# Reordering the small matmuls of a chunked recurrence on TensorE: one row size at a time, heads and blocks in turn

## The chip, the cores and the metric

The kernel runs on one core of one Trainium2 chip. The metric is the time of one execution in microseconds (us) on the device; lower is better. All times below are of this one core.

## What is computed

One layer of a hybrid decoder for 1024 prompt tokens and 8 sample tokens. What matters here is mixer B, a recurrence over tokens for 8 heads of 64 (the reference, cut):

```python
def wkv7_scan(r, decay, k, v, kk, a, S0):
    def step(S, inp):
        r_t, d_t, k_t, v_t, kk_t, a_t = inp
        sa = jnp.einsum('bhvk,bhk->bhv', S, -kk_t)
        S = S * d_t[:, :, None, :] + sa[..., None] * (kk_t * a_t)[:, :, None, :] + v_t[..., None] * k_t[:, :, None, :]
        y = jnp.einsum('bhvk,bhk->bhv', S, r_t)
        return S, y
```

Around it stand a projection `h @ w_in`, a second mixer (gated by a 128x128 matrix per head), `@ w_out`, a cross attention over 256 memory tokens and a squared-relu feed-forward, all in float32.

## The kernel before

Phase 1 (until about 780 us) makes the projections and both mixers, phase 2 the rest. All large products go through one helper, `gemm` (line 132): float32 is split into a high and a low part, and three exact-part matmuls of 128x128 weights by 256 to 512 columns are issued per 128 rows of the contraction; these have the output `ps_g` or, for the memory, `ps_kv`.

The recurrence is done by chunks of 64 tokens, in two halves of 512 tokens, for pairs of heads: a head lies on 64 partitions, a pair on 128. Per half there are four pairs; two pairs (`q`) share an inverse and a chain. The parts, all plain float32, so that each matmul in the code is two passes in the trace (two weight loads and two MATMUL records):

- `gram` (line 494, output `psgram`): products of the factors inside each chunk; weights 64 rows x 128 columns.
- `inverse` and `join` (lines 574 to 597, `ps_j`): a DVE routine inverts 16x16 blocks, then five sets of 32x32x32 products join them to 64x64. Each of four blocks b lies on 32 partitions; `tile_position` puts it on that part of the array. 224 matmuls per join, four joins.
- `fold` (line 609, `psf`): 64x64x64 products with the inverse, 8 chunks x 2 heads per call, 16 calls.
- `chain` (lines 622 and 630, `psx`, `psz`): the recurrence itself, chunk by chunk, two matmuls of 128 rows x 64 columns per head and chunk with copies by ACT and DVE between; not touched.
- `outs` (lines 647 and 648, `psy`): per chunk and head one matmul with 128 rows of weights (line 647) and one with 64 rows (line 648) into the same 64x64 of PSUM; 128 of each in the program.

The list `ORDER` sets the priority of these parts. The order on each engine is then laid out by the framework's scheduler, so that parts run into each other on PE, which executes its matmuls in that order. The small matmuls' outputs lie in PSUM pools of two buffers: `pm` (gram, join and others) and `py` (fold, outs, one product of join and others).

Of the kernel before, what the change touches and what calls it, by code (L numbers as in the profile page):

```python
# [9 lines left out]
F32 = mybir.dt.float32  # L10
# [6 lines left out]
PSUM = bass.MemoryType.PSUM  # L17
DRAM = bass.MemoryType.DRAM

P = 128  # L20
# [42 lines left out]
def order():  # L63
    """phase 1 in the order in which its parts take precedence: names and arguments (half, pair or head, part)."""
    parts = (p.split() for p in ORDER.replace("\n", " ").split(","))
    return [(name, *map(int, args)) for name, *args in parts]


class K:
# [25 lines left out]
    # ---------------------------------------------------------------- helpers  # L95
# [14 lines left out]
    def load_w(self, src, g=None, eng=None, st=None):  # L110
        """src: [1024, 128] of DRAM (or st: loaded) -> hi and lo [128, 8, 128]."""
        nc = self.nc
        st = st or self.w_tile(src)
        if g is not None:
            nc.gpsimd.tensor_tensor(st, st, g.unsqueeze(2).broadcast_to([P, KT, P]), op=ALU.mult)  # L115
        wh = self.wp.tile([P, KT, P], F32R, tag="wh", name="wh")
        wl = self.wp.tile([P, KT, P], F32R, tag="wl", name="wl")
        self.split(wh, wl, st, eng=eng or nc.gpsimd)
        return wh, wl

    def gemm(self, ps, w, xh, xl, cols, kt=KT):
        """ps += w^T x over kt tiles, in three exact-part passes."""
# [11 lines left out]
    def rsqrt_small(self, out, ss, scale, eps, shape, pool):  # L134
        """out = 1/sqrt(ss*scale + eps): a first guess from the exponent's bits, three Newton steps."""
# [12 lines left out]
    def rsqrt(self, v, y, t):  # L148
        """v -> 1/sqrt(v) in y (v [128, n] kept); t: scratch."""
# [81 lines left out]
    # ---------------------------------------------------------------- phase 1  # L231
# [34 lines left out]
    def x_store(self, hf, i):  # L266
        """tile i of 128 tokens: x^T to d_x (of the second half, ahead of its turn, with the sum of squares)."""
# [19 lines left out]
    def x_scale(self, rs, c0):  # L287
        """rb from column c0 on: 1 / rms (a column of rs per tile of tokens) over the partitions."""
# [65 lines left out]
    def proj(self, hf, col0, dst, sdst):  # L354
        """dst[128, 512] (and sdst[128, 8]) = rstd * (x g)^T w_in columns, for the half's tokens."""
# [13 lines left out]
    def shifted(self, hf, mi, out):  # L369
        """out[128, 512]: projected rows of m-tile mi after the token shift."""  # L370
# [11 lines left out]
    def loras(self, hf, i):  # L382
        """inputs of the decay and a low-rank maps (i = 0), of the gate's (1)."""
# [18 lines left out]
    def rkv(self, hf, pr, i):  # L402
        """r, k or v (i) of a pair of heads."""
# [5 lines left out]
    def kknorm(self, hf, pr):  # L409
        """unit-norm removal keys of both heads of the pair."""  # L410
# [12 lines left out]
    def lora(self, ps, fs, i):  # L423
        """the decay's (i = 0) or a's low-rank map: its input's high and low parts lie in one tile's halves."""
# [4 lines left out]
    def decay(self, hf, pr):  # L429
        """per-chunk cumulative decays lam, their inverses il, and tanh of the a-gate."""  # L430
# [22 lines left out]
    def factors(self, hf, pr):  # L453
        """decay-scaled factors: st = [-kk lam | r lam], bk = [kk a / lam | k / lam], and the bonus."""
# [21 lines left out]
    def gram(self, hf, pr):  # L476
        """masked products of the factors inside each chunk."""
# [9 lines left out]
        for cg in range(2):  # L487
            for h in range(2):
                hr = slice(64 * h, 64 * h + 64)
                orr = slice(64 - 64 * h, 128 - 64 * h)  # L490
                psg = self.pm.tile([P, 4, P], F32, tag="m", name="psgram")
                for ci in range(4):
                    c = cg * 4 + ci
                    nc.tensor.matmul(psg[:, ci, :], bk[hr, c].rearrange("p j t -> p (j t)"), st[hr, c, h, :], start=True, stop=True)  # L494
                cc = slice(cg * 4, cg * 4 + 4)
# [14 lines left out]
    def values(self, hf, pr):  # L510
        """values by token zv, with the state in the chain's first chunk."""
# [14 lines left out]
    def ends(self, hf, pr):  # L526
        """chunk-end factors e by token, in the place of the chunks' bk."""
# [11 lines left out]
    def inverse(self, hf, q):  # L539
        """(I - N)^-1 of the diagonal 16x16 blocks of two pairs, one problem per partition."""  # L540
# [18 lines left out]
    def join(self, hf, q):  # L559
        """16x16 -> 32x32 -> 64x64 inverses: D + D L D with L the blocks above the diagonal ones."""  # L560
# [23 lines left out]
        ps3 = self.py.tile([P, NS, 32], F32, tag="y", name="ps_j3")  # L584
        for h in range(2):
            r1, r2 = rows[2 * h], rows[2 * h + 1]
            for c in range(NS):
                nc.tensor.matmul(ps3[r2, c, :], wj[r2, c, :], nb[r2, c, :], start=True, stop=True, tile_position=(64 * h + 32, 64 * h + 32))
            self.copy(("vector", "scalar")[h])(dt[r2], ps3[r2])
            for c in range(NS):  # L590
                ab = self.s[prs[c // NCH]]["ab"]
                nc.tensor.matmul(ps2[r2, c, :], ab[r1, c % NCH, 32:64], tt[r1, c, 0:32], start=True, stop=True, tile_position=(64 * h, 64 * h + 32))
            self.copy("scalar" if h else "vector")(wj[r2], ps2[r2])
        for h in range(2):
            r2 = rows[2 * h + 1]
            for c in range(NS):
                nc.tensor.matmul(ps3[r2, c, :], dt[r2, c, :], wj[r2, c, :], start=True, stop=True, tile_position=(64 * h + 32, 64 * h + 32))
            nc.vector.tensor_copy(tt[r2, :, 0:32], ps3[r2])

    def fold(self, hf, pr, i):  # L600
        """the inverse's product with the chunk-end factors (i = 0) or the outputs' ones (1), in their place."""
# [3 lines left out]
        for h in range(2):  # L605
            hr = slice(64 * h, 64 * h + 64)
            dst = t["e"][hr, 0:NCH, h, :] if i == 0 else t["ab"][hr, :, C:]
            for c in range(NCH):
                nc.tensor.matmul(ps[hr, c, :], tt[hr, c, :], dst[:, c, :], start=True, stop=True)  # L609
            self.copy((("vector", "scalar"), ("scalar", "scalar"))[i][h])(dst, ps[hr])  # L610

    def chain(self, hf, q, c0, c1):
        """chunks c0..c1 of the recurrence of two pairs."""
# [21 lines left out]
    def outs(self, hf, pr):  # L635
        """the recurrence's outputs by token, less their mean over each head."""
# [16 lines left out]
    def gn_core(self, y, n, sq, rs, pool, tag):  # L653
        """y -> (y - mean) / sqrt(var + eps) over the 64 partitions of each head."""
# [34 lines left out]
    # ---------------------------------------------------------------- sample tokens of mixer B  # L689
# [124 lines left out]
    # ---------------------------------------------------------------- mixer A  # L814
# [16 lines left out]
    def layernorm(self, x, n, rows, h):  # L831
        """x [rows, n, 128] normalised in place over the last axis; h: the head of the n groups (None: one each)."""
# [23 lines left out]
    def proj_a(self, hf, h, i):  # L856
        """v (i = 0) or u (1) of head h, before the gelu; the gelu of both after u."""
# [54 lines left out]
    # ---------------------------------------------------------------- states out, memory keys and values  # L912
# [17 lines left out]
    def mem_norm(self):  # L930
        """normalised memory tokens, feature-major, to d_m."""
# [30 lines left out]
    def memkv(self, i, m0, m1):  # L962
        """feature tiles m0..m1 of the memory's keys (i = 0) or values (1)."""
# [21 lines left out]
    # ---------------------------------------------------------------- phase 2  # L985
# [3 lines left out]
    def tile_cols(i):  # L989
        """columns of the i-th tile of 128 prompt tokens; tile 8: the sample tokens."""  # L990
# [5 lines left out]
    def halves(self, b0, b1):  # L996
        """the half of x (hi, lo) with columns b0..b1, and their slice in it."""
# [3 lines left out]
    def residual(self, m, x, b0, b1, first):  # L1001
        """x (columns b0..b1 of feature tile m) -> hi and lo; adds x^2 to the sums."""
# [10 lines left out]
    def phase2(self, phases):  # L1013
# [5 lines left out]
        with ExitStack() as c2:  # L1019
            # each pool lies on the bytes of one of phase 1 (o0: sb, x0: xp, x1: sa), and waits for that one alone  # L1020
# [62 lines left out]
    def token_ms(self, tiles, pool):  # L1083
        """sums of squares by token, in the columns of a PSUM tile."""
# [5 lines left out]
    def token_rs(self, tiles):  # L1090
        """1 / (16 rms) by token, in columns of rs (sample tokens: rs8)."""
# [16 lines left out]
    def attention(self, h, grps):  # L1108
        """head h of the cross attention for groups of 256 prompt tokens (with group 1: the sample tokens)."""
# [54 lines left out]
    def softmax(self, ps, n, scale, pool):  # L1164
        """rows of ps [n, 256]: softmax(ps * scale), scale > 0 (an AP [n, 1] or 1.0)."""
# [12 lines left out]
    def sample_head(self, h, qs):  # L1178
        """head h of the cross attention of the sample tokens over their cached memories."""
# [182 lines left out]
```

## Time and profile before

| | us |
|---|---|
| median of 3 runs | 1934.5 (1933.2 to 1941.1) |
| span of the profiled execution, first to last instruction | 1928.3 |
| what lies around the span, against the median | 6.2 |
| PE busy | 1837.6 (95%) |
| DVE busy | 1027.4 (53%) |
| ACT busy | 634.2 (33%) |
| POOL busy | 631.0 (33%) |

No device time of the profiled execution itself is on its page beside the span, so the span stands for it, and the 6.2 us to the median for what lies around it. A matmul's record runs from its start to the modelled end of its result, so records of neighbours overlap, and the step from one start to the next is what a matmul takes from the engine. Idle time is listed with what ended it.

### The profile page before, as it was taken

To read this page: it belongs to the slowest core of one execution; us is meant where nothing else is said; L and a number is where in the kernel's file an instruction comes from. 1 tells how busy PE (TensorE), PEld (TensorE's weight loads), DVE (VectorE), ACT (ScalarE), POOL (GpSimd) and SP (SyncE) were. 2 spreads that over 40 slices of the span, in tenths; PEclk is the share of its full clock that TensorE was granted. 3 is DMA by queue.
4 is the path that set the end of the run, shared out by engine and by line. 5 is a ranking of instruction groups with operands and counts; after the bars stand their busy time and mean duration, and the time that the engine had idled before them with its cause. 6 is when DMAs were issued, how large, how long until landed. Compare 5 with 4: busy or idle time off the path is not lost.

```text
span 1928.3 us, 33970 instructions
## 1 busy us (share of the span) xinstructions
PE 1837.6 (95%) x13965; PEld 1632.4 (85%) x13965; DVE 1027.4 (53%) x2123; ACT 634.2 (33%) x1254; POOL 631.0 (33%) x530
## 2 busy tenths in 40 slices
PE   6989998999998979999999999999999999999998
PEld 6888787988887778888888798899999999998998
DVE  5794677557867764565666558333332323232335
ACT  4534443353353324343333332221212131312133
POOL 6540242204435654366442154120202121212110
PEclk8998885898998778999999999999999999999999
DMA  4312322121222346355544111111111111120212
GB/s 140 100 57 83 86 75 64 54 58 34 73 69 64 110 144 188 88 180 153 170 143 153 34 55 50 34 55 39 55 41 53 51 39 52 41 68 23 66 45 89
DMA packets 235884, 152.84 MB, mean 79 GB/s; under 512 B 20616, under 2 KB 219680, under 8 KB 235728
## 3 DMA queue, kind: packets, MB, share of 16 engines
q1 hardware_dynamic: 235684, 150.65, 26.1%
q8 instruction: 110, 1.80, 0.4%
q14 instruction: 46, 0.38, 0.1%
q10 hardware_dynamic: 44, 0.01, 0.0%
HBM read 131.07 MB, written 19.56 MB: 78 GB/s over the span
## 4 chain that ended last, share of the span: by engine, by line
PE 77%; DVE 13%; issue 3%; DMA 3%; POOL 2%; ACT 2%; DVEq 0%; SPq 0%; POOLq 0%; ACTq 0%
PE ps_g L132 57%; PE psy L648 2%; PE psf L609 2%; PE ps_kv L132 2%; PE psy L647 2%; PE ps_so L1220 2%; PE ps_j L574 1%; DVE ptmp L553 1%; PE psx L622 1%; PE psgram L494 1%; PE ps_j L581 1%; DMA qb<-d_q 1%; DVE pb L554 1%; PE ps_o L1157 1%; DVE st L466 1%
## 5 line engine op out<-in xcount | busy, mean ns | idle before, releaser
L132 PE MATMUL ps_g<-x,wh 128*128 128x260 f32 (+3 forms) x2048 | 444.3, 311 | 3.1 <-ACT rl L1269 3.0
L132 PEld LDWEIGHTS ps_g<-x,wh 128*128 128x128 f32 x2048 | 333.5, 188 | 29.6 <-ACT rl L1269 4.5
L132 PE MATMUL ps_g<-x,wl 128*128 128x260 f32 (+3 forms) x1024 | 316.6, 310 | 0.0
L99 ACT CAST wh<-wst 128x1024 fp32r<-128x1024 f32 x124 | 129.8, 1048 | 282.9 <-PE ps_g L132 197.8
L132 PE MATMUL ps_g<-xh,wh 128*128 128x256 f32 (+1 forms) x704 | 215.4, 306 | 5.4 <-ACT xr L284 1.8
L132 PE MATMUL ps_g<-sl,wdh 128*128 128x260 f32 (+1 forms) x672 | 211.5, 320 | 0.0
L132 PE MATMUL ps_g<-sh,wdh 128*128 128x260 f32 (+1 forms) x672 | 211.4, 320 | 0.0
L132 PE MATMUL ps_g<-xl,wh 128*128 128x256 f32 (+1 forms) x704 | 209.2, 297 | 0.5 <-DVE xl L100 0.5
L132 PE MATMUL ps_g<-xh,wl 128*128 128x256 f32 (+1 forms) x704 | 209.3, 298 | 0.0
L100 POOL TENSOR_TENSOR wl<-wst,wh 128x1024 fp32r<-128x1024 f32 x70 | 170.4, 2434 | 107.5 <-ACT wh L99 97.3
L1283 DVE TENSOR_TENSOR acc<-ps_g,acc 128x260 f32<-128x260 f32 (+1 forms) x200 | 98.9, 500 | 199.1 <-PE ps_g L132 199.1
L132 PE MATMUL ps_g<-sh,wdl 128*128 128x260 f32 (+1 forms) x672 | 204.5, 320 | 0.0
L132 PEld LDWEIGHTS ps_g<-x,wl 128*128 128x128 f32 x1024 | 192.1, 188 | 11.8
L115 POOL TENSOR_TENSOR wst<-wst,prm 128x1024 f32<-128x1024 f32 x40 | 76.1, 1904 | 329.3 <-DMA wst<-in_w_up_dram 149.2
L132 PE MATMUL ps_g<-o,wh 128*128 128x260 f32 (+1 forms) x768 | 178.3, 326 | 3.1 <-DVE xn L1054 1.8
L1271 POOL TENSOR_TENSOR rl<-rl 128x260 f32<-128x260 f32 (+1 forms) x96 | 76.3, 796 | 247.7 <-ACT sh L1270 247.3
L132 PEld LDWEIGHTS ps_g<-xh,wh 128*128 128x128 f32 x704 | 140.8, 200 | 12.8 <-issue 4.4
L132 PEld LDWEIGHTS ps_g<-xl,wh 128*128 128x128 f32 x704 | 140.7, 200 | 4.9 <-issue 1.9
L132 PEld LDWEIGHTS ps_g<-o,wh 128*128 128x128 f32 x768 | 129.2, 191 | 16.6 <-issue 3.1
L132 PEld LDWEIGHTS ps_g<-xh,wl 128*128 128x128 f32 x704 | 139.9, 199 | 3.3 <-issue 1.0
L132 PEld LDWEIGHTS ps_g<-sh,wdh 128*128 128x128 f32 x672 | 126.0, 188 | 10.2
L132 PEld LDWEIGHTS ps_g<-sh,wdl 128*128 128x128 f32 x672 | 124.0, 188 | 11.0
(443 smaller groups left out, 3559.7 us busy)
## 6 DMA issues: line engine op xcount, KB each, us to landing
wst<-in_w_in_dram SPq DMA_DIRECT2D x44, 512.0 KB
wst<-in_w_up_dram SPq DMA_DIRECT2D x32, 512.0 KB
wdst<-in_w_down_dram SPq DMA_DIRECT2D x64, 256.0 KB
wst<-in_w_out_dram SPq DMA_DIRECT2D x16, 512.0 KB
ck<-in_cache_mem_k_dram SPq DMA_DIRECT2D x32, 256.0 KB
ck<-in_cache_mem_v_dram SPq DMA_DIRECT2D x32, 256.0 KB
sbv<-d_sv SPq DMA_DIRECT2D x40, 128.0 KB
xt<-in_x_prompt_dram SPq DMA_DIRECT2D x8, 512.0 KB
```

Of the source, the lines that this page charges most:

```text
L99: (heng or nc.scalar.copy)(hi, src)
L100: (eng or nc.vector).tensor_tensor(lo, src, hi.bitcast(F32), op=ALU.subtract)
L115: nc.gpsimd.tensor_tensor(st, st, g.unsqueeze(2).broadcast_to([P, KT, P]), op=ALU.mult)
L132: nc.tensor.matmul(ps, l[:, k, :], r[:, cols], start=(k == 0 and i == 0), stop=(k == kt - 1 and i == 2))
L466: nc.vector.scalar_tensor_tensor(st[hr, :, h, 0:64], cs3(kkn[hr, :]), -1.0, lam[hr, :, 0:C], op0=ALU.mult, op1=ALU.mult)
L494: nc.tensor.matmul(psg[:, ci, :], bk[hr, c].rearrange("p j t -> p (j t)"), st[hr, c, h, :], start=True, stop=True)
L609: nc.tensor.matmul(ps[hr, c, :], tt[hr, c, :], dst[:, c, :], start=True, stop=True)
L647: nc.tensor.matmul(dst, st[:, c, h, 64:128], zv[:, c, h, :], start=True, stop=False, tile_position=(0, r0))
L648: nc.tensor.matmul(dst, ab[hr, c, 64:128], uv[hr, (c - 1) % (NCH + 1), h, :], start=False, stop=True, tile_position=(64 * h, r0))
L1220: nc.tensor.matmul(po, pt[:, t, b, :], vts[b // 2][:, b % 2, t, :], start=(n == 0), stop=(n == 15))
L1271: nc.gpsimd.tensor_tensor(r[:, 0:n], r[:, 0:n], r[:, 0:n], op=ALU.mult)
L1283: nc.vector.tensor_tensor(acc[:, m, b0:b1], ps, acc[:, m, b0:b1], op=ALU.add)
```

## The change

The same matmuls are issued in another order, and the copies out of PSUM move behind them. `outs` takes both heads together: for each head the eight 128-row matmuls, then the sixteen 64-row ones with the two heads in turn; both heads' PSUM buffers are held at once. `gram` and `fold` take the two heads in turn for each chunk, `join` its blocks in turn for each chunk; the copies that stood between the heads or blocks stand after the last matmul. Comment lines and docstrings go too.

```diff
 gram:
         for cg in range(2):
-            for h in range(2):
-                psg = self.pm.tile([P, 4, P], F32, tag="m", name="psgram")
-                for ci in range(4):
+            psgs = [self.pm.tile([P, 4, P], F32, tag="m", name="psgram") for h in range(2)]
+            for ci in range(4):
+                for h in range(2):
...
 join:
-        for b, rr in enumerate(rows):
-            for c in range(NS):
+        for c in range(NS):
+            for b, rr in enumerate(rows):
                 nc.tensor.matmul(ps1[rr, c, :], self.s["nl"][rr, c, :], pt[rr, c, :], start=True, stop=True, tile_position=(32 * b, 32 * b))
...
+        for c in range(NS):
+            for b, rr in enumerate(rows):
+                nc.tensor.matmul(ps2[rr, c, :], nb[rr, c, :], wj[rr, c, :], start=True, stop=True, tile_position=(32 * b, 32 * b))
         for b in (0, 2, 1, 3):
-            rr = rows[b]
-            for c in range(NS):
-                nc.tensor.matmul(ps2[rr, c, :], nb[rr, c, :], wj[rr, c, :], start=True, stop=True, tile_position=(32 * b, 32 * b))
-            self.copy("scalar" if b > 1 else "vector")(tt[rr, :, b % 2 * 32:b % 2 * 32 + 32], ps2[rr])
+            self.copy("scalar" if b > 1 else "vector")(tt[rows[b], :, b % 2 * 32:b % 2 * 32 + 32], ps2[rows[b]])
...
 fold:
-        for h in range(2):
-            hr = slice(64 * h, 64 * h + 64)
-            dst = t["e"][hr, 0:NCH, h, :] if i == 0 else t["ab"][hr, :, C:]
-            for c in range(NCH):
+        for c in range(NCH):
+            for hr, dst in zip(hrs, dsts):
                 nc.tensor.matmul(ps[hr, c, :], tt[hr, c, :], dst[:, c, :], start=True, stop=True)
...
 outs:
-        for h in range(2):
-            hr = slice(64 * h, 64 * h + 64)
-            psy = self.py.tile([P, NCH // 2, C], F32, tag="y", name="psy")
+        psys = [self.py.tile([P, NCH // 2, C], F32, tag="y", name="psy") for h in range(2)]
+        for h, psy in enumerate(psys):
             for c in range(NCH):
                 r0 = c % 2 * 64
-                dst = psy[r0:r0 + 64, c // 2, :]
-                nc.tensor.matmul(dst, st[:, c, h, 64:128], zv[:, c, h, :], start=True, stop=False, tile_position=(0, r0))
-                nc.tensor.matmul(dst, ab[hr, c, 64:128], uv[hr, (c - 1) % (NCH + 1), h, :], start=False, stop=True, tile_position=(64 * h, r0))
+                nc.tensor.matmul(psy[r0:r0 + 64, c // 2, :], st[:, c, h, 64:128], zv[:, c, h, :], start=(c < 2), stop=False, tile_position=(0, r0))
+        for c in range(NCH):
+            r0 = c % 2 * 64
+            for h, hr in enumerate(hrs):
+                nc.tensor.matmul(psys[h][r0:r0 + 64, c // 2, :], ab[hr, c, 64:128], uv[hr, (c - 1) % (NCH + 1), h, :], start=False, stop=(c >= NCH - 2), tile_position=(64 * h, r0))
```

After the change the lines of `join` are 576 to 603, of `fold` 616, of `chain` 630 and 638, of `outs` 655 and 659; numbers behind a name tell buffers apart.

PE at the last outputs of the third pair of the second half, before (the outputs of one head, `psy_6314`, after the fold that they wait for):

```order
L609 MATMUL psf_6173<-ab_4990,tt_5075 64x64 x8
L648 MATMUL psy_6314<-bk_4939,ab_4990 64x64
L647 MATMUL psy_6314<-zv_5334,st_4938 64x64
L648 MATMUL psy_6314<-bk_4939,ab_4990 64x64
L647 MATMUL psy_6314<-zv_5334,st_4938 64x64
```

PE at the same place after the change (`psy_6314` and `psy_6315` are the two heads of the pair):

```order
L616 MATMUL psf_6173<-ab_4990,tt_5075 64x64 x16
L494 MATMUL psgram_6485<-st_6297,bk_6298 128x128 x3
L494 MATMUL psgram_6486<-st_6297,bk_6298 128x128
L655 MATMUL psy_6314<-zv_5334,st_4938 64x64 x8
L494 MATMUL psgram_6486<-st_6297,bk_6298 128x128
L659 MATMUL psy_6314<-bk_4939,ab_4990 64x64
L655 MATMUL psy_6315<-zv_5334,st_4938 64x64 x8
L659 MATMUL psy_6315<-bk_4939,ab_4990 64x64
L659 MATMUL psy_6314<-bk_4939,ab_4990 64x64
L659 MATMUL psy_6315<-bk_4939,ab_4990 64x64
```

The 128-row and the 64-row matmuls took turns one by one; now eight of the first kind stand in a row, and the second kind follows with the heads in turn.

PE in the last join of phase 1, before (`ps_j2` and `ps_j3` are two of its products, and `ps_kv` are matmuls of `gemm` that stand between its blocks):

```order
L132 MATMUL ps_kv_7905<-xh_6875,wl_7902 128x256
L581 MATMUL ps_j2_7023<-wj_7021,nb_970 32x32 x16
L588 MATMUL ps_j3_7093<-nb_970,wj_7021 32x32 x16
L977 MATMUL ps_kvt_7932<-ident_115,kvt_7930 128x128 x2
L132 MATMUL ps_kv_7945<-xh_6872,wh_7941 128x256
```

PE at the same join after the change:

```order
L132 MATMUL ps_kv_7689<-xh_6875,wl_7686 128x256
L582 MATMUL ps_j2_7023<-wj_7021,nb_970 32x32 x64
L590 MATMUL ps_j3_7093<-nb_970,wj_7021 32x32 x32
L989 MATMUL ps_kvt_7717<-ident_115,kvt_7714 128x128 x2
L132 MATMUL ps_kv_7825<-xh_6872,wh_7821 128x256
```

What came in four pieces of 16 with matmuls of `gemm` between them comes in one piece of 64, with the four blocks in turn inside it, and the 32 of the next product directly behind.

## Rows read from the trace of the kernel before

**Rows 1.** The page: busy time; the chain that ended last, by engine and line.

```profile
PE 1837.6 (95%) x13965; PEld 1632.4 (85%) x13965; DVE 1027.4 (53%) x2123; ACT 634.2 (33%) x1254; POOL 631.0 (33%) x530
PE 77%; DVE 13%; issue 3%; DMA 3%; POOL 2%; ACT 2%; DVEq 0%; SPq 0%; POOLq 0%; ACTq 0%
PE ps_g L132 57%; PE psy L648 2%; PE psf L609 2%; PE ps_kv L132 2%; PE psy L647 2%; PE ps_so L1220 2%; PE ps_j L574 1%; DVE ptmp L553 1%; PE psx L622 1%; PE psgram L494 1%; PE ps_j L581 1%; DMA qb<-d_q 1%; DVE pb L554 1%; PE ps_o L1157 1%; DVE st L466 1%
```

**Rows 2.** Stretches: length, each engine's busy us (x instructions), clock share, DMA.

```profile
0.00:780.00 780.00, 714.14 (x6521) 625.35 (x6522) 526.91 (x1185) 317.41 (x610) 314.96 (x301) 0.87 0.30 88
400.00:500.00 100.00, 98.05 (x714) 82.44 (x714) 70.52 (x129) 44.53 (x88) 31.55 (x35) 0.93 0.17 50
600.00:700.00 100.00, 80.91 (x530) 67.85 (x528) 83.53 (x162) 32.23 (x68) 68.78 (x52) 0.74 0.37 110
```

**Rows 3.** Groups by line on PE: names, shapes, xcount | busy us, mean ns | idle before.

```profile
L648 PE MATMUL psy<-bk,ab 64*64 64x64 f32 x256 | 48.0, 275 | 0.0
L647 PE MATMUL psy<-zv,st 128*64 128x64 f32 x256 | 45.1, 271 | 2.9 <-DVE zv L633 2.9
L494 PE MATMUL psgram<-st,bk 64*128 64x128 f32 x256 | 40.1, 324 | 5.0 <-DVE st L497 3.4 <-DVE rs_s L142 0.9 <-POOL lc L451 0.6
L574 PE MATMUL ps_j<-pt,nl 32*32 32x32 f32 x512 | 22.1, 220 | 9.2 <-DVE pt L557 8.2 <-DVE rs_t L145 0.9
L581 PE MATMUL ps_j<-wj,nb 32*32 32x32 f32 x512 | 22.0, 203 | 0.0
L609 PE MATMUL psf<-ab,tt 64*64 64x64 f32 x256 | 19.5, 222 | 1.0 <-DVE y L651 1.0
L609 PE MATMUL psf<-bk,tt 64*64 64x64 f32 x256 | 17.3, 228 | 1.8 <-DVE bk L610 1.8
```

**Rows 4.** Timeline of PE from 799.9 us: start, us, instruction, records merged.

```profile
799.90 0.33 PE L647 MATMUL psy<-zv,st 128*64 128x64 f32 x2
800.16 0.33 PE L648 MATMUL psy<-bk,ab 64*64 64x64 f32 x2
```

**Rows 5.** Timeline of PE inside another run of outputs.

```profile
466.68 0.47 PE L647 MATMUL psy<-zv,st 128*64 128x64 f32 x2
467.08 0.47 PE L648 MATMUL psy<-bk,ab 64*64 64x64 f32 x2
```

**Rows 6.** Timeline of PE: whole runs of folds (x16, x32) and joins.

```profile
356.70 1.14 PE L609 MATMUL psf<-bk,tt 64*64 64x64 f32 x16
...
361.02 1.78 PE L609 MATMUL psf<-bk,tt 64*64 64x64 f32 x32
...
347.10 1.19 PE L592 MATMUL ps_j<-tt,ab 32*32 32x32 f32 x32
...
522.85 3.93 PE L574 MATMUL ps_j<-pt,nl 32*32 32x32 f32 x128 [0.93 <-DVE rs_t L145]
```

**Rows 7.** Stretches, instructions on `psy` alone: PE, weight loads, DVE, clock, DMA.

```profile
259.00:276.00 17.00, 11.14 (x64) 7.80 (x64) 0.69 (x2) 0.66 0.16 47
461.00:472.00 11.00, 10.34 (x64) 7.42 (x64) 0.51 (x2) 0.72 0.00 0
634.00:648.00 14.00, 11.47 (x62) 8.03 (x62) 0.85 (x2) 0.59 0.30 85
799.90:812.30 12.40, 8.49 (x64) 6.16 (x64) 1.26 (x3) 0.86 0.22 64
```

**Rows 8.** The chain that ended last, 799 to 813 us, by line.

```profile
by line: PE ps_g L132 40.1%; PE psy L648 30.1%; PE psy L647 29.6%; PE psz L630 1.9%
```

**Rows 9.** The same chain around 229 us: start, us, what.

```profile
226.91 0.22 ACT bk L623
...
228.55 0.27 DVE zv L633
```

**Rows 10.** DVE copies of the joins: duration ns min/median/max, first and last start.

```profile
L582 DVE COPY tt<-ps_j x8: 678/681/684, 154.3 to 718.8; 32x512 f32<-32x512 f32 x8
```

More of the change, by code (lines that the diff above doesn't have):

```diff
@@ L487, in gram @@
         for cg in range(2):
-            for h in range(2):
+            cc = slice(cg * 4, cg * 4 + 4)
+            psgs = [self.pm.tile([P, 4, P], F32, tag="m", name="psgram") for h in range(2)]
+            for ci in range(4):
+                c = cg * 4 + ci
+                for h in range(2):
+                    hr = slice(64 * h, 64 * h + 64)
+                    nc.tensor.matmul(psgs[h][:, ci, :], bk[hr, c].rearrange("p j t -> p (j t)"), st[hr, c, h, :], start=True, stop=True)
+            for h, psg in enumerate(psgs):
                 hr = slice(64 * h, 64 * h + 64)
                 orr = slice(64 - 64 * h, 128 - 64 * h)
-                psg = self.pm.tile([P, 4, P], F32, tag="m", name="psgram")
-                for ci in range(4):
-                    c = cg * 4 + ci
-                    nc.tensor.matmul(psg[:, ci, :], bk[hr, c].rearrange("p j t -> p (j t)"), st[hr, c, h, :], start=True, stop=True)
-                cc = slice(cg * 4, cg * 4 + 4)
                 nc.vector.tensor_tensor(ab[hr, cc, :], psg[hr], mk[hr], op=ALU.mult)
@@ L583, in join @@
         dt = self.sb.tile([P, NS, 32], F32, tag="ta", name="dt")
         ps3 = self.py.tile([P, NS, 32], F32, tag="y", name="ps_j3")
+        for c in range(NS):
+            for h in range(2):
+                r2 = rows[2 * h + 1]
+                nc.tensor.matmul(ps3[r2, c, :], wj[r2, c, :], nb[r2, c, :], start=True, stop=True, tile_position=(64 * h + 32, 64 * h + 32))
         for h in range(2):
-            r1, r2 = rows[2 * h], rows[2 * h + 1]
-            for c in range(NS):
-                nc.tensor.matmul(ps3[r2, c, :], wj[r2, c, :], nb[r2, c, :], start=True, stop=True, tile_position=(64 * h + 32, 64 * h + 32))
@@ L589, in join @@
-            self.copy(("vector", "scalar")[h])(dt[r2], ps3[r2])
-            for c in range(NS):
-                ab = self.s[prs[c // NCH]]["ab"]
+            self.copy(("vector", "scalar")[h])(dt[rows[2 * h + 1]], ps3[rows[2 * h + 1]])
+        for c in range(NS):
+            ab = self.s[prs[c // NCH]]["ab"]
+            for h in range(2):
+                r1, r2 = rows[2 * h], rows[2 * h + 1]
                 nc.tensor.matmul(ps2[r2, c, :], ab[r1, c % NCH, 32:64], tt[r1, c, 0:32], start=True, stop=True, tile_position=(64 * h, 64 * h + 32))
-            self.copy("scalar" if h else "vector")(wj[r2], ps2[r2])
@@ L594, in join @@
         for h in range(2):
-            r2 = rows[2 * h + 1]
-            for c in range(NS):
+            self.copy("scalar" if h else "vector")(wj[rows[2 * h + 1]], ps2[rows[2 * h + 1]])
+        for c in range(NS):
+            for h in range(2):
+                r2 = rows[2 * h + 1]
                 nc.tensor.matmul(ps3[r2, c, :], dt[r2, c, :], wj[r2, c, :], start=True, stop=True, tile_position=(64 * h + 32, 64 * h + 32))
-            nc.vector.tensor_copy(tt[r2, :, 0:32], ps3[r2])
+        for h in range(2):
+            nc.vector.tensor_copy(tt[rows[2 * h + 1], :, 0:32], ps3[rows[2 * h + 1]])
@@ L604, in fold @@
         ps = self.py.tile([P, NCH, C], F32, tag="y", name="psf")
-        for h in range(2):
-            hr = slice(64 * h, 64 * h + 64)
-            dst = t["e"][hr, 0:NCH, h, :] if i == 0 else t["ab"][hr, :, C:]
-            for c in range(NCH):
+        hrs = (slice(0, 64), slice(64, 128))
+        dsts = [t["e"][hr, 0:NCH, h, :] if i == 0 else t["ab"][hr, :, C:] for h, hr in enumerate(hrs)]
+        for c in range(NCH):
+            for hr, dst in zip(hrs, dsts):
                 nc.tensor.matmul(ps[hr, c, :], tt[hr, c, :], dst[:, c, :], start=True, stop=True)
+        for h, (hr, dst) in enumerate(zip(hrs, dsts)):
             self.copy((("vector", "scalar"), ("scalar", "scalar"))[i][h])(dst, ps[hr])
@@ L640, in outs @@
         t["y"] = y = self.sl.tile([P, HALF], F32, tag="y", bufs=2, name="y")
-        for h in range(2):
-            hr = slice(64 * h, 64 * h + 64)
-            psy = self.py.tile([P, NCH // 2, C], F32, tag="y", name="psy")
+        hrs = (slice(0, 64), slice(64, 128))
+        psys = [self.py.tile([P, NCH // 2, C], F32, tag="y", name="psy") for h in range(2)]
+        for h, psy in enumerate(psys):
             for c in range(NCH):
                 r0 = c % 2 * 64
-                dst = psy[r0:r0 + 64, c // 2, :]
-                nc.tensor.matmul(dst, st[:, c, h, 64:128], zv[:, c, h, :], start=True, stop=False, tile_position=(0, r0))
-                nc.tensor.matmul(dst, ab[hr, c, 64:128], uv[hr, (c - 1) % (NCH + 1), h, :], start=False, stop=True, tile_position=(64 * h, r0))
+                nc.tensor.matmul(psy[r0:r0 + 64, c // 2, :], st[:, c, h, 64:128], zv[:, c, h, :], start=(c < 2), stop=False, tile_position=(0, r0))
[3 more added lines that the diff above has]
+                nc.tensor.matmul(psys[h][r0:r0 + 64, c // 2, :], ab[hr, c, 64:128], uv[hr, (c - 1) % (NCH + 1), h, :], start=False, stop=(c >= NCH - 2), tile_position=(64 * h, r0))
+        for h, psy in enumerate(psys):
             nc.vector.tensor_reduce(sm[:, h], psy, axis=AX.X, op=ALU.add)
```

## The prediction, made before the changed kernel was run

> **What bounds the kernel now.** The page first: PE is busy 95% of the span, and it holds 77% of the chain that ended last, in which the small lines of the recurrence stand beside `gemm`: the two lines of `outs`, `fold`, the products of `join`, `gram` [rows 1]. Then the stretches: all of these lie in the first 780 us, where PE is busy 714 us and DVE 527; between 400 and 500 us PE is busy 98 of 100, and only between 600 and 700 does DVE lead, 83.5 to 81, at a mean clock of 0.74 [rows 2]. So phase 1 is bound by PE nearly throughout, with little idle time, but with DVE close enough to take over in places. Phase 2 issues the same matmuls in the same order as before, and I give it nothing.
>
> Busy time hides what a small matmul costs, since a record includes its way out of the array (some 0.2 us); the step from one start to the next is what counts. The groups give the sizes: `outs` 48.0 and 45.1 us, the first two products of `join` 22.1 and 22.0, `fold` 19.5 and 17.3, `gram` 40.1 [rows 3].
>
> The timeline gives the prices. Where 128-row and 64-row matmuls of `outs` take turns, each (two passes) starts 0.26 us after the one before [rows 4]; at half clock, 0.40 us [rows 5]. Eight `fold` matmuls of one size and one head, 16 passes, take 1.14 us; less the 0.22 us of the last record this is 0.115 us each [rows 3, 6]. So in `outs` over half of each step is spent on the change of row count. Sixteen 32-row matmuls take 1.19 us; less 0.20 us, 0.062 each [rows 3, 6].
>
> Two longer runs show what happens where neighbours lie on other rows of the array. Two such `fold` runs end to end would take 2.06 us; sixteen matmuls with two boundaries between heads took 1.78, so a boundary gave back 0.14 us. Four 32-row runs end to end would take 4.16 us; the 64 matmuls of one `ps_j` tile, with three boundaries between blocks, took 3.93, so a boundary gave back 0.08 us [rows 6]. At a boundary the next head's or block's first matmuls run beside the last ones of the other, a little over one matmul's time each. The change makes nearly every matmul such a boundary.
>
> **The change part by part.**
>
> *Outs.* I counted the order on PE over both programs: of the 256 matmuls 218 follow one with another array shape before, 49 after. Two kinds of place differ.
>
> First, the four dense runs, one per couple of pairs: 254 records, 127 matmuls, 11.14 + 10.34 + 11.47 + 8.49 = 41.4 us, at mean clocks of 0.59 to 0.86 [rows 7]. After the change these places hold 16 changes of shape, at 0.26, and some 112 matmuls without one. Those take at most 0.115 us, if nothing overlaps, and at least 0.058, half of that, if neighbours always do; rows or columns of the array alternate for nearly all, the boundary above sits close to full overlap for rows, and I assume the same for columns: 0.07. That is 12 us at full clock, some 16 at the clock of before: 14, so 27 us less. These runs are on the chain: in the last one `outs` is 60% of 14 us [rows 8]; one of the four lies in DVE's stretch. I count 85%: **-23 us**.
>
> Second, the other 129 matmuls, laid between the steps of the recurrence: 129 x 0.26 = 33.5 us before; after, 33 changes of shape at 0.26 and 96 at 0.07, 15 us. There PE often waits for the step's copies and update anyway (0.22 us on ACT, 0.27 on DVE stand on the chain itself [rows 9]), so a third of the 18 us: **-6 us**.
>
> *Joins.* 896 matmuls at 0.062 are 56 us, more in stretches at half clock. With two blocks at a time they cost half, 0.031; with four, 0.016; with no overlap, 0.062. Nearest to the boundary row is two at a time, so 0.035: 24 us less. `gemm` work of PE fills the time around them, so it can be used, but a part of each join is followed by copies that PE waits for; 75%: **-18 us**.
>
> Here a rule speaks against the change. The Trainium skill, TensorEngine Tiling, "Restrictions and Gotchas", says that different row tiles cannot access the same PSUM bank at the same time; all blocks of a join write one bank, and so do both heads of a fold. By it joins and folds would gain nothing. The run of 64 above is one tile in one bank and still gave time back at its boundaries, so for this kernel I go by the row; the rule's result is a rival below.
>
> *Folds.* 256 matmuls from 0.115 to 0.07: 11.5 us less, 80% on the path: **-9 us**. The bounds are 0 and 14.6.
>
> *Gram.* The scheduler keeps most heads apart: 21 of 128 matmuls stand next to one of the other head, against 9 before. Twelve at 0.1 us, about half of two passes: **-1 us**.
>
> *What it adds.* Copies that ran beside the next block's matmuls now wait for the last one. In a join a DVE copy is 0.68 us [rows 10], two in a row twice per join: 2.7 us, 11 over the four. The order places some 22 to 32 `gemm` matmuls behind each product, which cover most of it; I charge 3. Behind the copies on DVE stand its evacuations of `gemm`, and PE's next `ps_g` waits for those. `gram` and `outs` hold both buffers of their pools until both heads are done, which delays the next user: 2. If the cover were gone, it would be the whole 11 and as much for `gram` and `outs`. **+5 us**.
>
> *Sum.* -23 - 6 - 18 - 9 - 1 + 5 = -52 us against the span of 1928.3: 1876. With the 6.2 us around the span, **1882 us**, against the median of 1934.5.
>
> **The rivals.**
>
> *PE's time is freed, but little reaches the end.* All of PE's savings together are 27 + 18 + 24 + 11.5 + 1, some 82 us. DVE is busy 527 of 780 us, and the recurrence's steps wait for copies [rows 2, 9]. If PE only waits longer for these, a third arrives: -27 + 5, so 1912. Against it: PE is at 98% where DVE is at 71% [rows 2]. 16%.
>
> *One bank at a time.* If blocks and heads that write one bank take turns there, joins and folds gain nothing, outs still do: -29 - 1 + 5, so 1909. This is what the rule of TensorEngine Tiling in the Trainium skill would do here. Against it stands the run of 64 [rows 6]. 6%.
>
> *More overlap, all on the path.* Four blocks at a time (0.02), folds at 0.058, outs' 45 us in full: -45 - 38 - 15 + 5, so about 1842. For it speaks the clock, which falls inside the dense runs [rows 5, 7]; shorter runs may keep it up for what follows. 12%.
>
> *Every hop costs: slower.* The change makes about 1176 hops between row groups where there were some 50. A long alternation may lose what a single boundary gives, if each hop has to load its weights afresh, as a change of shape does (0.26 - 0.115 = 0.145 us). With three quarters on the path, 1176 x 0.77 x the cost stands against the 25 us that outs and gram, less the added waits, still give: it decides from 0.028 us per hop on. At 0.145 it would be 131 us, and 2041 in all. Against it: the boundaries in the trace gave time back, none took any [rows 6]. 4%.
>
> **How the numbers follow.** My forecast has 62%, and by itself a range of 1862 to 1902, from the bounds of the overlap and of the shares on the path. With the rivals at 16, 6, 12 and 4%, a range of 1842 to 1918 leaves out the slow rival, half of the fastest one and the end of the first. A measurement of this kernel can tell about 0.5% (10 us) from no change: faster means under 1925. My forecast, the fast rival and the bank rule fall there, and most of the first rival: 89%. Within 0.5%: the rest of the first rival and the least of the bank rule, 6%. Slower: the hops, and a mishap of the new order, 5%.
>
> **What would show it.** Right: runs of `psy` at lines 655 and 659 with steps of 0.06 to 0.12 us between equal lines; a join's first 64 matmuls in about 2.3 us where it was 3.9; sixteen folds in about 1.2 us where it was 1.8; psy off the last chain's list; `ps_g` lines unchanged in count and price. The span shrinks before 780 us and not behind. Wrong: joins still at 3.9 us (the bank rule); PE's idle time in phase 1, 66 us now (780 - 714), growing by most of what was saved (the first rival); steps of 0.1 us and more inside a join (the hops); a lower clock in phase 1 than the 0.87 of now [rows 2], which would raise `gemm`'s price there.

## The result and the profile after

The changed kernel takes **1866.8 us** (median of 4 runs, 1860.8 to 1870.7) against 1936.4 (1933.2 to 1941.1) for the kernel before: a ratio of 0.965, 95% interval 0.9617 to 0.9682, so some 68 us less. The prediction was 1882 us with a range of 1842 to 1918. The profiled execution has a device time of 1867.8 us and a span of 1866.1, so 1.7 us lie around the span. One execution of a kernel told below, the change less folds, took 4119 us where its other three took 1863 to 1865, and stands in no ratio.

The page after: busy time and the chain that ended last.

```profile
PE 1735.4 (93%) x13965; PEld 1545.9 (83%) x13965; DVE 1026.5 (55%) x2123; ACT 631.3 (34%) x1253; POOL 625.8 (34%) x530
PE 73%; DVE 13%; DMA 4%; issue 4%; ACT 3%; POOL 2%; SPq 0%; DVEq 0%; POOLq 0%; ACTq 0%
PE ps_g L132 59%; PE ps_kv L132 2%; PE ps_so L1232 2%; PE psgram L494 1%; DMA qb<-d_q 1%; DVE ptmp L555 1%; PE ps_o L1169 1%; PE psx L630 1%; POOL ck L1212 1%; DVE pb L556 1%; DVE st L466 1%; PE ps_sc L1155 1%; PE psz L638 1%; DVE sp L1187 1%; PE psf L616 1%
```

PE has the same 13965 instructions and is busy 102.2 us less than in [rows 1], while the span is 62.2 us shorter: 40 us of what was freed became idle time (90.7 us of the span before, 130.7 now). `psy` and `ps_j`, which stood in the chain's list, are gone from it.

Groups by line on PE after, columns as in [rows 3].

```profile
L494 PE MATMUL psgram<-st,bk 64*128 64x128 f32 x256 | 40.8, 322 | 15.6 <-DVE st L499 14.8 <-POOL lc L451 0.4 <-DVE bk L471 0.4
L655 PE MATMUL psy<-zv,st 128*64 128x64 f32 x256 | 23.1, 254 | 3.6 <-DVE zv L641 3.3
L659 PE MATMUL psy<-bk,ab 64*64 64x64 f32 x256 | 13.8, 263 | 2.7 <-ACT ab L618 2.7
L616 PE MATMUL psf<-ab,tt 64*64 64x64 f32 x256 | 12.7, 236 | 7.8 <-DVE y L663 7.8
L616 PE MATMUL psf<-bk,tt 64*64 64x64 f32 x256 | 9.0, 220 | 0.0
L576 PE MATMUL ps_j<-pt,nl 32*32 32x32 f32 x512 | 6.1, 209 | 11.6 <-DVE pt L559 11.6
L582 PE MATMUL ps_j<-wj,nb 32*32 32x32 f32 x512 | 5.4, 193 | 0.2 <-issue 0.2
```

The first two products of the joins fell from 22.1 and 22.0 us to 6.1 and 5.4, the outputs from 45.1 and 48.0 to 23.1 and 13.8, the folds from 36.8 to 21.7; `gram` stayed. The mean of one record hardly moved (220 to 209 ns for `ps_j`): the records overlap more, and a view that gives only the mean of one would show no change. The idle column grew where PE waits for DVE: 5.0 to 15.6 us ahead of `gram`, 1.0 to 7.8 ahead of a fold.

The same after as stretches (columns as in [rows 2]).

```profile
0.00:720.00 720.00, 613.17 (x6470) 537.72 (x6471) 526.93 (x1183) 313.80 (x608) 307.56 (x300) 0.88 0.32 94
500.00:600.00 100.00, 76.09 (x759) 64.98 (x760) 72.90 (x189) 36.38 (x81) 55.90 (x42) 0.80 0.21 64
```

DVE's 526.9 us, which filled 780 us before [rows 2], are now done in 720; PE is busy 613 of these. Between 500 and 600 us PE and DVE are both near 75%, and PE's two longest waits for DVE lie there, 7.8 us ahead of a fold and 12.7 ahead of `gram`. The last output matmul starts at 741.6 us, before at 812.1; from there to the end it is 1124.5 us against 1116.2, so phase 2 gave nothing: some 7264 PE records start from the last output on where 7199 did, so some `gemm` work that stood ahead of it now stands behind it, and 8 of the 70 us go to that.

Three places in the timeline of PE after: a join's first two products and a fold, and the last outputs.

```profile
143.47 1.59 PE L576 MATMUL ps_j<-pt,nl 32*32 32x32 f32 x128 [2.89 <-DVE pt L559]
150.12 1.27 PE L582 MATMUL ps_j<-wj,nb 32*32 32x32 f32 x126
165.84 2.08 PE L616 MATMUL psf<-bk,tt 64*64 64x64 f32 x64
729.27 0.33 PE L655 MATMUL psy<-zv,st 128*64 128x64 f32 x2
729.53 0.32 PE L659 MATMUL psy<-bk,ab 64*64 64x64 f32 x2
730.16 0.67 PE L659 MATMUL psy<-bk,ab 64*64 64x64 f32 x26
736.57 0.69 PE L655 MATMUL psy<-zv,st 128*64 128x64 f32 x16
```

Less the last record, the 126 passes of a join take 1.08 us: 8.6 ns a pass or 17 ns a matmul, where [rows 6] had 62 ns. The fold's 64 passes take 1.86 us, 58 ns a matmul (115 before). The 64-row outputs take (0.67 - 0.22) / 26 = 17 ns a pass, 35 ns a matmul; the 128-row ones (0.69 - 0.22) / 16 = 29 ns a pass, 59 ns a matmul. A change of row count still costs 0.26 us (729.27 to 729.53), as in [rows 4]. The single starts in the trace show the overlap: from 150.175 us on, the join's records start in fours, 7 ns apart inside a four and 32 ns from one four to the next; the 64-row outputs from 730.267 us on start in fours too, 58 ns from one four to the next.

The step sums of phase 1 in us, worked out from all of PE's starts up to 20 us behind the last output (each matmul's step to the next start; idle time is included there, and listed once more in the last column):

| | gemm | gram | psx | psz | joins | folds | outs 128 rows | outs 64 rows | idle |
|---|---|---|---|---|---|---|---|---|---|
| before | 429 | 42.8 | 32.9 | 21.0 | 68.4 | 35.4 | 37.0 | 42.2 | 61 |
| after | 428 | 51.6 | 37.8 | 32.3 | 32.9 | 20.5 | 21.8 | 12.7 | 102 |

Joins, folds and outs gave back 35.5 + 14.9 + 44.7 = 95 us; `gram` and the recurrence's `psx` and `psz` took 25 of these again; `gemm`'s sum is unchanged, though with 2742 matmuls in this stretch where there were 2802. That is the 70 us by which the last output came earlier; at the end of the span 62 of them are left.

### The profile page after: what moved, and what is told of

Read it like the earlier page. It is cut to its first block, busy times and chain, and to the rows that moved or that the text cites. A ratio compares the mean times of both kernels' runs of the same rounds, so it can differ in the third digit from the quotient of the medians.

```text
span 1866.1 us, 33959 instructions
## 1 busy us (share of the span) xinstructions
PE 1735.4 (93%) x13965; PEld 1545.9 (83%) x13965; DVE 1026.5 (55%) x2123; ACT 631.3 (34%) x1253; POOL 625.8 (34%) x530
## 4 chain that ended last, share of the span: by engine, by line
PE 73%; DVE 13%; DMA 4%; issue 4%; ACT 3%; POOL 2%; SPq 0%; DVEq 0%; POOLq 0%; ACTq 0%
PE ps_g L132 59%; PE ps_kv L132 2%; PE ps_so L1232 2%; PE psgram L494 1%; DMA qb<-d_q 1%; DVE ptmp L555 1%; PE ps_o L1169 1%; PE psx L630 1%; POOL ck L1212 1%; DVE pb L556 1%; DVE st L466 1%; PE ps_sc L1155 1%; PE psz L638 1%; DVE sp L1187 1%; PE psf L616 1%
## 5 line engine op out<-in xcount | busy, mean ns | idle before, releaser
L132 PE MATMUL ps_g<-xl,wh 128*128 128x256 f32 (+1 forms) x704 | 213.5, 303 | 1.1 <-DVE xl L100 1.1
L1284 DVE TENSOR_TENSOR sl<-rl,sh 128x260 fp32r<-128x260 f32 (+1 forms) x96 | 50.1, 525 | 154.3 <-POOL rl L1283 154.3
```

The costliest lines, as they stand in the source:

```text
L132: nc.tensor.matmul(ps, l[:, k, :], r[:, cols], start=(k == 0 and i == 0), stop=(k == kt - 1 and i == 2))
L1284: nc.vector.tensor_tensor(sl[:, 0, b0:b1], r[:, 0:n], sh[:, 0, b0:b1].bitcast(F32), op=ALU.subtract)
```

## The experiments

Times are medians; ratios are to the kernel before, run on the same chip, and where us of a part are told, they are worked out from the ratios.

### One part of the change at a time

Each is the kernel before with one function of the change and the other three as they were. Outs alone:

```diff
-        for h in range(2):
-            hr = slice(64 * h, 64 * h + 64)
-            psy = self.py.tile([P, NCH // 2, C], F32, tag="y", name="psy")
+        psys = [self.py.tile([P, NCH // 2, C], F32, tag="y", name="psy") for h in range(2)]
+        for h, psy in enumerate(psys):
...
+        for c in range(NCH):
+            r0 = c % 2 * 64
+            for h, hr in enumerate(hrs):
...
```

> Only outs is changed; gram, join and fold as before. Theory (the gain comes from what PE spends per small matmul, part by part): psy falls from 79 us of PE steps to some 35, as with the whole change; with most of it on the path the time is 25 to 45 us below before, 1892 to 1912. Rival (the freed time is swallowed by DVE and the copies, and the whole change gains only where its parts come together): under 15 us, 1922 or more.

Joins alone:

```diff
-        for b, rr in enumerate(rows):
-            for c in range(NS):
+        for c in range(NS):
+            for b, rr in enumerate(rows):
...
```

> Only join is changed. Theory: the joins' steps fall from 68 us to some 33, four blocks running beside each other; 15 to 30 us below before, 1907 to 1922. Rival (hidden: gemm fills the time, so the joins were not on the path): under 7 us, 1930 or more, though the joins' steps fall all the same.

Folds alone:

```diff
-        for h in range(2):
...
-            for c in range(NCH):
+        for c in range(NCH):
+            for hr, dst in zip(hrs, dsts):
...
+        for h, (hr, dst) in enumerate(zip(hrs, dsts)):
...
```

> Only fold is changed. Theory: folds' steps fall from 35 us to some 20; 6 to 15 us below before, 1922 to 1931. Rival: nothing that can be told, 1932 to 1940.

Gram alone:

```diff
-            for h in range(2):
-                psg = self.pm.tile([P, 4, P], F32, tag="m", name="psgram")
-                for ci in range(4):
+            psgs = [self.pm.tile([P, 4, P], F32, tag="m", name="psgram") for h in range(2)]
+            for ci in range(4):
+                for h in range(2):
...
```

> Only gram is changed; both of pm's buffers are held until both heads are done. Theory: PE gains nothing, since few heads stand next to each other in the order, and waits longer for DVE's evacuations: 0 to 10 us above before, 1936 to 1946. Rival (gram gains like the others): 8 us or more below, under 1929.

| | us | ratio | PE busy in the profile |
|---|---|---|---|
| outs alone | 1911.8 | 0.9909 (0.9882 to 0.9936) | 1808.7 |
| joins alone | 1912.8 | 0.9917 (0.9892 to 0.9942) | 1799.1 |
| folds alone | 1950.6 | 1.0105 (1.0053 to 1.0157) | 1855.2 |
| gram alone | 1931.7 | 1.0002 (0.9969 to 1.0036) | 1854.7 |

Outs give 18 us and joins 16, as the two theories had it, with step sums (36.1 us for the outputs, 36.2 for the joins) close to those that they named. Gram gives nothing, the least of what its theory allowed, and the folds' order alone makes the kernel 20 us slower, which neither its theory nor its rival had; that rests on four runs that spread over 21 us. The four sum to some 13 us gained, against 68 in the whole change: the parts don't add up.

### Why the folds alone are slower

In the profile of folds alone, the fold steps fell as they should (35.4 to 23.9 us), yet PE is busy 17.6 us longer than before. The stretch to 840 us of the kernel before, columns as in [rows 2].

```profile
0.00:840.00 840.00, 774.14 (x6991) 679.74 (x6992) 563.04 (x1251) 342.57 (x664) 345.18 (x323) 0.88 0.31 91
```

The same stretch with folds alone, and a piece of it.

```profile
0.00:840.00 840.00, 765.52 (x6809) 668.83 (x6810) 550.83 (x1228) 332.36 (x643) 324.77 (x312) 0.83 0.29 85
625.00:673.00 48.00, 38.36 (x217) 30.24 (x214) 36.23 (x69) 12.93 (x28) 31.86 (x28) 0.50 0.18 52
```

The granted clock of the stretch is 0.83, where it was 0.88: more time at the lower of the two levels (0.50, 1.2 GHz), where every matmul costs more: an output's step is 0.26 us above it and 0.40 at it [rows 4, 5]. One piece at that level lasts from 625 to 673 us; ahead of it, from 620 to 625 us, PE had run the recurrence's short matmuls with waits of 0.49, 0.79 and 0.27 us for DVE between them. The test keeps the copies where folds alone had them and puts the matmuls back head by head:

```diff
-        for c in range(NCH):
-            for hr, dst in zip(hrs, dsts):
+        for hr, dst in zip(hrs, dsts):
+            for c in range(NCH):
                 nc.tensor.matmul(ps[hr, c, :], tt[hr, c, :], dst[:, c, :], start=True, stop=True)
```

> The kernel before with the fold's matmuls head by head as before, but the copies of both heads behind the matmuls of both, as the alternating fold has them. So it has the dependencies of the fold-only run without its order of matmuls. Theory: the fold-only run was slower because the later copies and the other order of the engines' work lengthen the waits and with them the stretches at the lower clock, not because of the matmuls themselves: as slow here, a ratio of 1.008 to 1.016. Rival: the alternation itself costs; then this one stands at 0.997 to 1.003.

Measured: 1932.1 us, ratio 0.9999 (0.9976 to 1.0021). The stretch to 840 us of this kernel:

```profile
0.00:840.00 840.00, 773.92 (x6928) 677.43 (x6929) 560.36 (x1245) 336.29 (x655) 336.84 (x320) 0.87 0.30 88
```

Its clock, 0.87, is close to that of before, and so is its time. The theory fell: the late copies cost nothing that shows. The rival, by its numbers, holds: with the turns the time rises, without them not. But the turns don't cost at their own place, since the fold steps got cheaper. The single runs tell more. By the mean granted clock of the span, in us, the runs at four levels of it (copies late on another chip than the rest):

| granted clock | before | folds alone | gram alone | copies late |
|---|---|---|---|---|
| 0.946 | 1926.3 | | 1923.4 | 1927.8, 1927.9, 1930.1 |
| 0.939 | 1932.5, 1938.4 | 1936.8 | 1933.0 | 1940.6 |
| 0.934, 0.933 | 1946.4 | 1944.5 | 1944.6 | |
| 0.926, 0.924 | | 1957.7, 1956.6 | | |

At the same clock the four kernels take the same time to within some 8 us, and each one's runs take longer the lower their clock is. So folds alone are slower by as much as their clock is lower. Why that order of instructions ends more often at the lower level isn't settled: the scheduler lays out the whole of PE's order anew for each kernel, so that the fold's turns could not be tried with everything else in place.

### The whole change less one part

Each is the changed kernel with one function as before. Less gram:

```diff
-            psgs = [self.pm.tile([P, 4, P], F32, tag="m", name="psgram") for h in range(2)]
...
+                psg = self.pm.tile([P, 4, P], F32, tag="m", name="psgram")
...
```

> The whole change without gram's part. Theory (gram's part makes PE wait for evacuations on DVE, 15 us of idle time before gram in the changed kernel against 5): 3 to 10 us below the changed kernel, a ratio to before of 0.960 to 0.9635. Rival (DVE has the same evacuations to do either way, so the wait only moves): the changed kernel's ratio, 0.965, within 0.002.

Less folds:

```diff
-            for hr, dst in zip(hrs, dsts):
...
+            for c in range(NCH):
...
```

> The whole change but the fold, which goes head by head as before. Theory: in the presence of the other parts the fold's order saves PE steps too (its steps summed to 20.5 us in the profile of the whole change and 35.4 before), so without it the time is 8 to 15 us above the whole change, a ratio to the kernel before of 0.969 to 0.973. Rival: the fold's order costs here what it cost alone, through the stretches at the lower clock; then leaving it out gains 5 to 20 us, a ratio of 0.955 to 0.962.

Less outs:

```diff
-                nc.tensor.matmul(psy[r0:r0 + 64, c // 2, :], st[:, c, h, 64:128], zv[:, c, h, :], start=(c < 2), stop=False, tile_position=(0, r0))
+                nc.tensor.matmul(dst, st[:, c, h, 64:128], zv[:, c, h, :], start=True, stop=False, tile_position=(0, r0))
+                nc.tensor.matmul(dst, ab[hr, c, 64:128], uv[hr, (c - 1) % (NCH + 1), h, :], start=False, stop=True, tile_position=(64 * h, r0))
...
```

> The whole change but the outputs, which go as before, 128-row and 64-row matmuls in turns. Theory: the outputs' order is worth more beside the other parts than alone (alone 18 us), because what it frees is then taken up: 30 to 45 us above the whole change, a ratio of 0.980 to 0.988. Rival: the parts add up, 18 to 20 us above it, a ratio of about 0.975.

Less folds and gram (outs and joins only):

```diff
-            psgs = [self.pm.tile([P, 4, P], F32, tag="m", name="psgram") for h in range(2)]
...
+                psg = self.pm.tile([P, 4, P], F32, tag="m", name="psgram")
...
-            for hr, dst in zip(hrs, dsts):
...
+            for c in range(NCH):
...
```

> The kernel before with the outputs' and the joins' new order, fold and gram as before. Theory: these two carry the whole gain, more together than the sum of the two alone: a ratio of 0.962 to 0.970. Rival: the two alone add up (0.991 and 0.992): a ratio of about 0.982.

| | us | ratio | PE busy in the profile |
|---|---|---|---|
| whole change | 1866.8 | 0.9650 (0.9617 to 0.9682) | 1735.4 |
| less gram | 1861.3 | 0.9626 (0.9599 to 0.9653) | 1730.3 |
| less folds | 1864.4 | 0.9628 (0.9586 to 0.9669) | 1755.1 |
| less outs | 1884.5 | 0.9730 (0.9680 to 0.9779) | 1767.2 |
| outs and joins only | 1881.8 | 0.9722 (0.9692 to 0.9752) | 1759.9 |

Gram or folds can be left out at no cost. Less gram, 0.9626 is its theory's number, but the interval holds the rival's too, and some 10 of the 15.6 us of idle time ahead of `gram` are still there with gram's order as before, so they don't belong to its held buffers alone. Without the folds' turns PE is busy 20 us longer and the time is the same, since its idle time, 1862.9 - 1755.1 = 108 us, is less by about as much than the whole change's 131: in these two profiles the PE time that the folds free is waited away. The folds' theory fell: the time isn't 8 to 15 us above. The rival's 0.962 lies within the interval and is not ruled out, and its mechanism has something for it: the three runs lie at a granted clock of 0.953 to 0.956, those of the whole change at 0.948 to 0.953. Outs are worth 16 us here and 18 alone, so the rival holds there. For outs and joins together neither number came out: they bring 54 us, more than the 34 of the two alone, less than the whole. Without folds and gram both, some 14 us are missing that neither misses alone. The clock doesn't explain these 14 us: at 0.948 to 0.951 the runs of outs and joins only lie at 1879 to 1885 us, of the whole change at 1866 to 1871. No version beats the changed kernel by more than a measurement can tell.

### Which overlap pays: rows, columns, blocks

The next three are the changed kernel with another order inside one part. Outs with the 64-row matmuls head by head, so that neighbours lie on other columns of the array but not on other rows:

```diff
-        for c in range(NCH):
-            r0 = c % 2 * 64
-            for h, hr in enumerate(hrs):
+        for h, hr in enumerate(hrs):
+            for c in range(NCH):
+                r0 = c % 2 * 64
...
```

> The whole change, but the 64-row matmuls of outs go head by head: neighbours differ in columns of the array, not in rows. Theory (what counts in outs is that the array's shape changes less often, and columns overlap as well as rows): psy's steps and the time as in the changed kernel, ratio 0.963 to 0.967. Rival (only rows overlap): the 64-row matmuls take 0.115 us instead of some 0.06, 7 us of PE more, 0.967 to 0.969.

Measured: 1866.9 us, 0.9655 (0.9626 to 0.9685), as the whole change and as the theory had it. Joins block by block, copies behind all blocks as in the change:

```diff
-        for c in range(NS):
-            for b, rr in enumerate(rows):
+        for b, rr in enumerate(rows):
+            for c in range(NS):
...
```

> The whole change, but the joins' matmuls go block by block again; the copies stay behind the last one. Theory (the joins' gain is that four blocks run beside each other): steps back to 60 us and more, 15 to 30 us above the changed kernel, ratio 0.973 to 0.981. Rival (the gain came from join's matmuls standing in one piece, and the copies behind it): within 5 us of the changed kernel, 0.963 to 0.968.

Measured: 1896.0 us, 0.9813 (0.9773 to 0.9853), at the upper end of the theory's range, with the joins' step sum back at 65.2 us. Outs with both heads' 128-row, then both heads' 64-row matmuls of one chunk, which halves the changes of row count in the code; in the order on PE it takes few away:

```diff
-        for h, psy in enumerate(psys):
-            for c in range(NCH):
...
-                nc.tensor.matmul(psys[h][r0:r0 + 64, c // 2, :], ab[hr, c, 64:128], uv[hr, (c - 1) % (NCH + 1), h, :], start=False, stop=(c >= NCH - 2), tile_position=(64 * h, r0))
+                nc.tensor.matmul(psys[h][r0:r0 + 64, c // 2, :], st[:, c, h, 64:128], zv[:, c, h, :], start=True, stop=False, tile_position=(0, r0))
+            for h, hr in enumerate(hrs):
+                nc.tensor.matmul(psys[h][r0:r0 + 64, c // 2, :], ab[hr, c, 64:128], uv[hr, (c - 1) % (NCH + 1), h, :], start=False, stop=True, tile_position=(64 * h, r0))
```

> The whole change, but outs goes chunk by chunk: the 128-row matmuls of both heads, then their 64-row ones. 191 of 256 follow a change of shape (218 before, 49 in the changed kernel). Theory (the price is that of the change of shape): psy's steps back to 60 to 75 us, 20 to 35 us above the changed kernel, ratio 0.975 to 0.983. Rival (the price was that of two matmuls on the same rows in a row): two heads in turn already give most of it back, within 8 us of the changed kernel.

Measured: 1880.1 us, 0.9725 (0.9696 to 0.9755). The outputs' step sum is back at 68.0 us, as the theory had it; the time lies between theory and rival. The timeline of PE, joins by block:

```profile
143.36 6.10 PE L576 MATMUL ps_j<-pt,nl 32*32 32x32 f32 x128 [2.86 <-DVE pt L559]
155.41 3.84 PE L582 MATMUL ps_j<-wj,nb 32*32 32x32 f32 x125
```

Outs by head, the same view:

```profile
728.80 0.96 PE L659 MATMUL psy<-bk,ab 64*64 64x64 f32 x28
```

Outs two by two:

```profile
740.32 0.33 PE L654 MATMUL psy<-zv,st 128*64 128x64 f32 x2
740.58 0.33 PE L656 MATMUL psy<-bk,ab 64*64 64x64 f32 x2
```

Block by block the same products take 3.84 and 6.10 us (the second figure, like the 1.59, mostly at the lower clock) where in turns they took 1.27 and 1.59, so the turns themselves, not the later copies, are the joins' gain. With columns alone in turn the 64-row outputs take (0.96 - 0.22) / 28 = 26 ns a pass, with rows and columns 17, and they start in pairs, 58 ns from one pair to the next, where those start in fours: two at a time and four. So the rival, 0.115 us a 64-row matmul (two passes), fell. The 9 ns a pass don't show in the total, since few such runs are dense: the 64-row outputs' step sum is 14.5 us against 12.7. Two by two there are still places at 0.26 us from one kind to the next, and some 14 us of the total are lost again.

## Why the prediction was right, point by point

**The forecast's time** came out 15 us too high, inside its own range of 1862 to 1902, with the mechanism right: neighbours on other parts of the array overlap, and most of what PE saves reaches the end. Its 82 us of savings on PE were 95 in the step sums, and its net share that arrives, 52 of 82 (63%), was 70 of 95 (74%) up to the last output and 62 of 95 (65%) at the end of the span. That the sum fits so well is luck in part: the terms erred in both directions, shares on the path too high for outs and folds and waits too small, against an overlap too low for the joins. Up to 4.5 us of the 15 come from the 6.2 us added for what lies around the span: in the execution after it is 1.7 us, and if it was as much before, the rest was only that the profiled execution was quicker than the median. The signs it named are there: equal lines of `psy` at 0.035 to 0.059 us a step, under the 0.06 named, sixteen folds at 58 ns each, `gemm` unchanged, a clock of 0.88 in the shorter phase 1, and nothing gained behind it.

**Outs, -23 and -6.** PE's saving was sized right: 27 + 18 = 45 us forecast, 44.7 measured; in part by luck, since the assumed 0.07 us a matmul was 0.035 and 0.059, and the step sums hold waits besides. The share on the path was too high: leaving outs out costs 16 us, outs alone bring 18, not 29. What failed is the step "I count 85%".

**Joins, -18.** The term was mis-sized: two blocks at a time were assumed because a boundary between two was all that the trace had, 0.035 us a matmul. All four run beside each other (the starts in fours), 0.017 us, and the step sum fell by 35.5 us, not 24. Beside the rest the turns are worth 0.9813 - 0.9650 of the time, 32 us; alone the joins' order brings 16. The forecast for a first product (2.3 us for 3.9) was 1.3 to 1.6.

**Folds, -9.** 58 ns a matmul is the lower bound taken, and 14.9 us of steps were freed, the bound of 14.6. But none of it reached the end: less folds takes the same time, and folds alone take longer, at a lower clock. "80% on the path" is the step that failed.

**Gram, -1** and nothing measured, alone or left out.

**Added waits, +5**: too small. PE's idle time in phase 1 grew by 41 us, of which the waits listed above take 10.6 ahead of `gram` and 6.8 ahead of one fold, which waits for the outputs' read of `psy`, a tile of the pool of two that both use. That the waits belong to the held pairs of buffers was only argued, and for `gram` the runs speak against it: with gram's order as before some 10 us of waits stay ahead of it, with outs by head, where gram holds both buffers, 3.4.

**The rivals.** *Little reaches the end* was right in kind (idle time grew by 41 us, where the forecast said 66 would grow by most of the saving) but not in size. *One bank at a time* fell: all four blocks of a join write one tile of one bank, at 8.6 ns a pass in turns and 29 block by block ((3.84 - 0.19) / 125). The Trainium skill, TensorEngine Tiling (Array Packing), "Restrictions and Gotchas", by which different row tiles cannot access one PSUM bank at a time, does not agree with these rows. *More overlap* was right for joins and folds, and its 1842 missed by what the waits took back. *Every hop costs* fell too: 17 ns a matmul in a row of hops.

**What it had not in view** is that the parts don't add up. The sum of four terms came out right as a sum, but outs and joins bring 18 and 16 us alone and 54 together, and the 14 us that are missing without folds and gram are there again with either. The order on all engines is laid out anew for every kernel, and the waits go with it; that these make the 14 us is argued, not shown.

## What to carry to other kernels

Small matmuls on parts of the array should be issued so that each neighbour lies on other rows and columns, and those of another row count in blocks: here that took PE's time for them to a half and, for four blocks, to a quarter. Price such a change by PE's steps, not by the mean of a record, and count only what is followed by no wait: a part whose PE time falls may bring nothing, as the folds did, or stand in a kernel that is slower at a lower clock. Where a scheduler places the instructions, try parts together, since each alone told neither its share nor its sign.

## What the runs showed that was not expected

Four 32x32 blocks on the array's diagonal, one output bank: 8.6 ns a pass in turns, 29 ns one block at a time. 64x64 matmuls: 57 ns a pass one at a time [rows 6], 29 with heads in turn, 17 with heads and columns in turn. One kernel's time follows its granted clock from run to run: folds alone took 1936.8 us at 0.939 and 1957.7 at 0.926, all with the same instructions in the same order on each engine.
